# The within-chunk part of a chunked recurrence, cut into units of one head and two chunks and moved to other PSUM banks

## The chip, the cores and the metric

One core of a Trainium2 chip runs the whole program in one launch. The metric is the device time of that core in microseconds (us).

## What is computed

The program is two transformer blocks on 512 tokens of width 1024, in float32. The change lies in the second block, in a gated delta rule (a linear recurrence) with 8 heads that runs in both directions. A context of 256 tokens is scanned ahead of the 512, so a head has six chunks of 128 tokens: chunks 0 and 1 are the context, chunks 2 to 5 are the tokens whose outputs are wanted. In the reference, cut to what matters (its chunk is 64 tokens, the kernel's is 128):

```python
a_mat = where(strict, (kb @ k.T) * decay, 0.0)          # per head and chunk
t_mat = triangular_solve(eye + a_mat, eye)              # lower, unit diagonal
u, w  = t_mat @ vb, t_mat @ (kb * exp(gc))
qk    = where(tri, (q @ k.T) * decay, 0.0)
def step(s, inp):                                       # over the chunks, one after the other
    v_new = u_i - w_i @ s
    o_i   = qd_i @ s + qk_i @ v_new
    s     = s * gl_i + kd_i.T @ v_new
```

## The kernel before, in words

The function `gdn` works through the 8 heads as four pairs. For each pair four helpers run, and their order in the program is: `states(pair)`, `inputs(pair + 1)`, `output(pair)` (the loop at 1552; for the last pair `tail()`, which is projections of the next stage, stands in the place of `inputs`). Both directions of both heads go together, so there are four independent recurrences at a time.

`inputs` makes q, k and v of a pair: projections on TensorE (line 234, 235 and 237: every float32 product is three matmuls with operands split in a high and a low part) into `pg` banks; a convolution over tokens, of which ScalarE does the eviction (1247 and 1248) and a Silu (1256), and VectorE does the taps (1254, eight for a head of k or v, four for a head of q); and transposes on TensorE (1284) into `pt` banks, evicted by ScalarE (1286, 1289).

`states` has four parts:

- **The within-chunk part** (1358 to 1387). TensorE makes k k' and k q' for each chunk (1364, 1366) and, with a pair of matmuls (1373 a broadcast of decays, 1374 a mask), the exponent; ScalarE takes its Exp (1376); VectorE multiplies (1378 to 1380). The results are `M` and `E`, one each for a head and direction. The diagonal 32 by 32 blocks of `M` go to a tile `X`, by ScalarE copies (1384) and VectorE transposes (1386).
- **The inversion** of those blocks (1390 to 1404), a chain of small VectorE instructions, 31 steps, with a transpose of the whole at its start (1390) and two at its end (1403, 1404).
- **The merge** of the blocks to inverses of 128 by 128, small matmuls (1418 to 1458).
- **The chunk steps** (1461 to 1518), six of them: products with the state (1474, 1476), with the inverse (1488), the state's update (1501) and the output (1504).

`output` projects the gate z, squares and normalises the result (1533 to 1538), transposes it (1541), multiplies (1543) and stores it.

PSUM has eight banks: `pg` two, `pt` two and `sc` four. Before, the within-chunk part takes its products from `sc` banks, which the merge and the chunk steps use too, and its exponents from `pt` and `sc`. `M` and `E` lie in pages named `w`, taken anew for each pair.

No engine's order is written out by hand except SyncE's: a scheduler orders the instructions of the other engines ahead of time, by dependences and by the buffers that are free. On the chip each engine then takes its own list in that order, and waits at the head of it. SyncE's list (all loads of weights) is the program's order.

## Time and profile before

| | |
|---|---|
| median of 3 runs | 2312.93 us (2308.7 to 2313.16) |
| the profiled execution | 2312.48 us; its span 2310.7 us, so 1.8 us lie around the span |
| busy: TensorE, VectorE, ScalarE, GpSimd | 2192.4, 1211.8, 980.3, 263.1 us |
| the recurrence, from the gates to the last merge | about 1006 to 1410 us of the span |

Engines: PE is TensorE, PEld its weight loads, DVE VectorE, ACT ScalarE, POOL GpSimd. A row of the timeline has the start, the time from the first start to the last end, the engine and line, operation, tiles, shapes and, in brackets, how long the engine sat idle before it and what released it. Names of tiles are the program's names or those of its pools: `a` and `w` are pages, `gvn`, `gr` operands of the chunk steps, `inv` the tiles `X`, `L` and `Y` of the inversion, `whi` and `wlo` the split weights. A matmul's own duration is longer than its distance to the next; where a row merges several, the time beyond the first, divided by the others, is the distance.

### The profile page before, as it was taken

The numbers are of one execution on the slowest core, as the hardware profiler recorded it, in microseconds if no ns is written. First come the engines' busy times: TensorE is split into PE (matmuls) and PEld (weight loads), VectorE is DVE, ScalarE is ACT, GpSimd is POOL, SyncE is SP. The second block draws the span as 40 slices with busy tenths as digits, with TensorE's granted clock in tenths as the row PEclk, the third lists the DMA queues.
The fourth block names the chain that finished last, engine by engine and source line by source line (L and its number), as shares of the span: only waits on it lengthen the run. The fifth ranks groups of instructions, "written<-read, shape, count | busy, mean of one in ns | idle before, by whom it ended". The sixth has DMA issues, their size and how long they took to land.

```text
span 2310.7 us, 38251 instructions
## 1 busy us (share of the span) xinstructions
PE 2192.4 (95%) x15367; PEld 1947.6 (84%) x15367; DVE 1211.8 (52%) x2740; ACT 980.3 (42%) x2022; POOL 263.1 (11%) x435
## 2 busy tenths in 40 slices
PE   8999999998899999899989897999999998999999
PEld 8889988897779889767777787888898888898988
DVE  4554444555443233559596967436776454434343
ACT  4443244444333233565555553545555224314221
POOL 0221100001000001201111110301110001010112
PEclk9999999999999999999999998999999999999999
DMA  5234485465672232422121310240112542323232
GB/s 172 81 126 135 161 298 197 137 199 180 215 233 96 91 104 89 154 71 93 47 92 47 97 47 15 74 136 25 31 40 86 182 141 78 96 88 100 93 100 92
DMA packets 195817, 262.05 MB, mean 113 GB/s; under 512 B 12343, under 2 KB 157495, under 8 KB 195639
## 3 DMA queue, kind: packets, MB, share of 16 engines
q1 hardware_dynamic: 188864, 244.61, 32.7%
q10 hardware_dynamic: 6775, 15.00, 1.8%
q8 instruction: 120, 1.97, 0.4%
q14 instruction: 58, 0.48, 0.1%
HBM read 223.39 MB, written 36.18 MB: 112 GB/s over the span
## 4 chain that ended last, share of the span: by engine, by line
PE 75%; issue 9%; DMA 5%; DVE 4%; ACT 4%; POOL 2%; SPq 0%; ACTq 0%; POOLq 0%; DVEq 0%
PE pg L234 16%; PE pg L235 15%; PE pg L237 15%; PE sc L234 4%; PE sc L235 4%; PE sc L237 4%; DMA whi<-parts 2%; PE pg L223 1%; PE pg L224 1%; DMA parts<-fraw 1%; PE pg L225 1%; PE sc L1488 1%; DMA fraw<-in_w_in 1%; DMA wraw<-in_w_kv_mem 1%; DVE wlo L179 1%
## 5 line engine op out<-in xcount | busy, mean ns | idle before, releaser
L179 DVE TENSOR_TENSOR wlo<-wraw,whi 128x1024 fp32r<-128x1024 f32 (+2 forms) x267 | 325.6, 1222 | 405.9 <-ACT whi L178 401.2
L234 PE MATMUL pg<-xhi,whi 128*128 128x512 f32 (+1 forms) x1104 | 428.9, 392 | 30.4 <-DMA whi<-parts 12.9
L178 ACT ACTIVATE whi<-wraw 128x1024 fp32r<-128x1024 f32 (+2 forms) x267 | 275.6, 1035 | 417.0 <-PE pg L235 351.2
L235 PE MATMUL pg<-xlo,whi 128*128 128x512 f32 (+1 forms) x1104 | 426.1, 389 | 0.0
L237 PE MATMUL pg<-xhi,wlo 128*128 128x512 f32 (+1 forms) x1104 | 291.4, 384 | 1.0 <-DMA wlo<-parts 1.0
L234 PEld LDWEIGHTS pg<-xhi,whi 128*128 128x128 f32 x1104 | 211.3, 192 | 77.6 <-ACT whi L178 14.5
L235 PEld LDWEIGHTS pg<-xlo,whi 128*128 128x128 f32 x1104 | 211.3, 192 | 37.1
L237 PEld LDWEIGHTS pg<-xhi,wlo 128*128 128x128 f32 x1104 | 203.2, 190 | 41.0 <-DMA wlo<-parts 2.3
L234 PE MATMUL pg<-whi,xhi 128*128 128x256 f32 (+1 forms) x608 | 159.0, 291 | 0.5 <-ACT a L980 0.3
L235 PE MATMUL pg<-whi,xlo 128*128 128x256 f32 (+1 forms) x608 | 157.7, 290 | 0.0
L234 PE MATMUL sc<-whi,a 128*128 128x256 f32 x560 | 141.8, 285 | 1.6 <-ACT whi L178 1.6
L235 PE MATMUL sc<-whi,a 128*128 128x256 f32 x560 | 141.4, 284 | 0.0
L234 PE MATMUL pg<-whi,a 128*128 128x256 f32 x560 | 140.8, 283 | 0.0
L235 PE MATMUL pg<-whi,a 128*128 128x256 f32 x560 | 140.7, 283 | 0.0
L234 PEld LDWEIGHTS pg<-whi,xhi 128*128 128x128 f32 x608 | 118.9, 196 | 5.0 <-ACT whi L178 3.1
L235 PEld LDWEIGHTS pg<-whi,xlo 128*128 128x128 f32 x608 | 118.6, 195 | 1.1 <-issue 0.8
L237 PE MATMUL pg<-wlo,xhi 128*128 128x256 f32 (+1 forms) x608 | 104.3, 290 | 12.2 <-DVE wlo L179 12.2
L234 PEld LDWEIGHTS sc<-whi,a 128*128 128x128 f32 x560 | 107.8, 193 | 2.1 <-ACT whi L178 1.8
L235 PEld LDWEIGHTS sc<-whi,a 128*128 128x128 f32 x560 | 107.8, 192 | 0.2
L234 PEld LDWEIGHTS pg<-whi,a 128*128 128x128 f32 x560 | 107.5, 192 | 0.1
L235 PEld LDWEIGHTS pg<-whi,a 128*128 128x128 f32 x560 | 107.5, 192 | 0.0
L929 POOL TENSOR_TENSOR a<-a,a 128x256 f32<-128x256 f32 x64 | 48.9, 764 | 510.9 <-DVE a L928 510.2
(474 smaller groups left out, 4582.7 us busy)
## 6 DMA issues: line engine op xcount, KB each, us to landing
wraw<-in_w_in SPq DMA_DIRECT2D x56, 512.0 KB, 5.3
fraw<-in_w_mod SPq DMA_DIRECT2D x48, 512.0 KB, 5.6
parts<-fraw SPq DMA_DIRECT2D x48, 512.0 KB, 3.9
wraw<-in_w_gate_up SPq DMA_DIRECT2D x44, 512.0 KB, 4.8
wraw<-in_w_mlp_in SPq DMA_DIRECT2D x32, 512.0 KB, 3.8
wraw<-in_w_mlp_out SPq DMA_DIRECT2D x32, 512.0 KB, 3.6
whi<-parts SPq DMA_DIRECT2D x26, 512.0 KB, 4.0
wlo<-parts SPq DMA_DIRECT2D x26, 512.0 KB
```

The lines of the kernel that those rows point to most:

```text
L178: nc.scalar.activation(hi, raw, AF.Copy)
L179: self.wlo_eng.tensor_tensor(lo, raw, hi.bitcast(F32), op=OP.subtract)
L223: mm(out, a[0], b[0], start=start, stop=False)
L224: mm(out, a[0], b[1], start=False, stop=False)
L225: mm(out, a[1], b[0], start=False, stop=stop)
L234: mm(out, A[k][0], B[k][0], start=start and k == 0, stop=False)
L235: mm(out, A[k][late], B[k][1 - late], start=False, stop=False)
L237: mm(out, A[k][1 - late], B[k][late], start=False, stop=stop and k == n - 1)
L929: nc.gpsimd.tensor_tensor(self.x[t][:, cs], self.x[t][:, cs], u, op=OP.add)
L1488: mm(kv[h][:, d, 0], M[h, d][:, c], r[h, d], start=True, stop=True)
```

## The change

The within-chunk part is done in units of one head and two chunks (`a` = 0, 2, 4), for both directions at once. A unit takes one bank of `pg` for its products k k' and k q' and one of `pt` for its exponents, and none of `sc`. An exponent's matmul covers 256 columns for each direction, where it was 256 or 512 before; the multiplications on VectorE cover 256 columns each. `E` and `M` are now eight tiles (four each) that are taken once, ahead of the loop over the pairs, from new pages `m`; the list `w` gets shorter. The copies and transposes to `X` still come after the three units of a head. Lines of the changed kernel behind this part are smaller by 2, those of `inputs` larger by 1.

```diff
--- before.py
+++ after.py
@@ -21,7 +21,7 @@
 T = 512
 NEG = -1.0e30
 PHASE_A = dict(a=((4, 18), (2, 16)))
-PHASE_B = dict(a=((3, 14), (2, 9)), w=((3, 4), (2, 7), (1.5, 4), (1, 3)))
+PHASE_B = dict(a=((3, 14), (2, 9)), m=((3, 4), (2, 4), (1, 2)), w=((2, 4), (1.5, 4)))
 PHASE_C = dict(a=((6, 6), (4, 4), (3, 3), (2, 5)), t=((3, 3), (2, 8)))
 PHASE_D = dict(a=((4, 21), (2, 20)))
 BANKS_A = dict(pt=2, sc=3, fl=1)
@@ -1237,6 +1237,7 @@
         X, L, Y = (self.hb.tile([128, 32, 32], F32, name="inv", tag=f"inv{k}") for k in range(3))
         tm = [con.tile([128, 136], F32, name=f"invt{v}") for v in range(2)]
         nc.gpsimd.memset(X, 0.0)
+        E, M = ({(h, d): self.page([n, 128], s="m") for h in range(2) for d in range(2)} for n in (4, 6))
 
         def conv(ps, tile):
 
@@ -1355,36 +1356,33 @@
                 return slice(32 * b, 32 * b + 32)
 
 
-            E, M = {}, {}
             for h in range(2):
-                pg = [self.bank([128, n, 128], "sc") for n in (2, 4)]
-                pk = self.bank([128, 4, 128], "sc")
-                for c in range(6):
-                    k = kT[h][:, c]
-                    mm(pg[c >= 2][:, c - 2 * (c >= 2)], k, k, start=True, stop=True)
-                    if c >= 2:
-                        mm(pk[:, c - 2], k, qT[h][:, (c - 2) * 128:(c - 1) * 128], start=True, stop=True)
-                for d in range(2):
-                    i = d * 8 + h0 + h
-                    ec, e = self.page([2, 128], s="w"), self.page([4, 128], s="w")
-                    for a, n in ((0, 2), (2, 4)):
-                        pe = self.bank([128, n, 128], "sc" if a else "pt")
-                        pf = pe.rearrange("p a b -> p (a b)")
-                        mm(pf, sel[:, i:i + 1].to_broadcast([64, 128]), g["rows"][:, a * 128:(a + n) * 128], start=True, stop=False)
-                        mm(pe, idb, msk[:, d, None, :].to_broadcast([128, n, 128]), start=False, stop=True)
-                        for c in range(n):
-                            act((e if a else ec)[:, c], pe[:, c], AF.Exp, bias=nb[h][:, a + c, d:d + 1])
-                    m = self.page([6, 128], s="w")
-                    dve.tensor_tensor(m[:, :2], ec, pg[0], op=OP.mult)
-                    dve.tensor_tensor(m[:, 2:], e, pg[1], op=OP.mult)
-                    dve.tensor_tensor(e, e, pk, op=OP.mult)
+                for a in (0, 2, 4):
+                    kq = self.bank([128, 4, 128], "pg")
+                    pe = self.bank([128, 2, 2, 128], "pt")
+                    for c in (a, a + 1):
+                        k = kT[h][:, c]
+                        mm(kq[:, c - a], k, k, start=True, stop=True)
+                        if a:
+                            mm(kq[:, 2 + c - a], k, qT[h][:, (c - 2) * 128:(c - 1) * 128], start=True, stop=True)
+                    for d in D2:
+                        i = d * 8 + h0 + h
+                        mm(pe[:, d].rearrange("p a b -> p (a b)"), sel[:, i:i + 1].to_broadcast([64, 128]), g["rows"][:, a * 128:(a + 2) * 128], start=True, stop=False)
+                        mm(pe[:, d], idb, msk[:, d, None, :].to_broadcast([128, 2, 128]), start=False, stop=True)
+                    for d in D2:
+                        e = E[h, d][:, a - 2:a] if a else self.page([2, 128], s="m")
+                        for c in (a, a + 1):
+                            act(e[:, c - a], pe[:, d, c - a], AF.Exp, bias=nb[h][:, c, d:d + 1])
+                        dve.tensor_tensor(M[h, d][:, a:a + 2], e, kq[:, :2], op=OP.mult)
+                        if a:
+                            dve.tensor_tensor(e, e, kq[:, 2:], op=OP.mult)
+                for d in D2:
                     for b in range(4):
-                        xb, mb = X[blk(b), lane[h, d]], m[blk(b), :, blk(b)]
+                        xb, mb = X[blk(b), lane[h, d]], M[h, d][blk(b), :, blk(b)]
                         if d == 0:
                             act(xb, mb, AF.Copy)
                         else:
                             dve.transpose(xb, mb)
-                    E[h, d], M[h, d] = e, m
 
 
             dve.transpose(L, X.rearrange("p n i -> p i n"))
```

The scheduler's order changes with it, in each of the pairs. Three places, of the second pair (`inv` and the numbers behind a name, the buffer numbers, aside; `pg`, `pt`, `sc` are banks):

TensorE in the within-chunk part. Before (1373 and 1374 are the exponents, 234 to 237 projections of the pair after):

```order
L234 MATMUL pg<-xhi,whi 128x512
L1373 MATMUL pt<-rg,sel_7304 128x256
L1374 LDWEIGHTS idb
L1374 MATMUL pt<-gmask,idb 128x256
L235 MATMUL pg<-xlo,whi 128x512
L237 MATMUL pg<-xhi,wlo 128x512 x2
L1373 MATMUL sc<-rg,sel_7304 128x512
L1374 LDWEIGHTS idb
L1374 MATMUL sc<-gmask,idb 128x512
```

And now, from the transposes of the output (1539, before 1541) on:

```order
L1539 MATMUL pt<-ident,w_10595 128x128 x4
L1539 MATMUL pt<-ident,w_10596 128x128 x4
L1365 MATMUL pg<-a_10964 128x128 x2
L1370 MATMUL pt<-rg,sel_7304 128x256
L1371 LDWEIGHTS idb
L1371 MATMUL pt<-gmask,idb 128x256
L1370 MATMUL pt<-rg,sel_7304 128x256
L1371 LDWEIGHTS idb
L1371 MATMUL pt<-gmask,idb 128x256
L1365 MATMUL pg<-a_10964 128x128
L1367 MATMUL pg<-a_11125,a_10964 128x128
```

(`a_10964` and `a_11125` are k and q.) All 20 products and 24 matmuls of the exponents now stand in one row, with no projection between them; 25 projection matmuls stood between them before (36 of 256 columns in the last pair). In the first pair the six transposes of the gates' decays are still among them.

TensorE between the last chunk step and the transposes of the output. Before (1504 is the last step, the rows are the second half of the gate's projection):

```order
L1504 MATMUL sc<-gvn,w_10178 128x128
L1504 MATMUL sc<-gvn,w_10200 128x128
L237 MATMUL pg<-xhi,wlo 128x512 x4
L234 MATMUL pg<-xhi,whi 128x512
L235 MATMUL pg<-xlo,whi 128x512
```

Now (1502 is the last step; `hc` and the three rows ahead of it are the v projection of the second head, 1285 transposes of v, `xhi` with `whi` behind them the whole of the gate's projection):

```order
L1502 MATMUL sc<-gvn,m_9509 128x128
L237 MATMUL pg<-xhi,wlo 128x512 x3
L234 MATMUL pg<-hc,whi 128x256
L235 MATMUL pg<-hc,whi 128x256
...
L237 MATMUL pg<-hc,wlo 128x256 x4
L1285 MATMUL pt<-ident,a_11226 128x128 x6
L234 MATMUL pg<-xhi,whi 128x512
L235 MATMUL pg<-xlo,whi 128x512
```

Where 16 projection matmuls lay between the last step and the first transposes of the output (20 in the pairs after), 75 do now (51 of 512 columns, 24 of 256), with 12 transposes of v. The ones that are new here stood among the chunk steps before; those now have matmuls of about the same length there from the q and v projections, which stood beside the inversion and the merge before. In the last pair 174 projection matmuls stand between the output and the merge in both kernels; 36 of them stood inside the within-chunk part before, and all stand behind it now.

VectorE at the same place. Before, the normalisation of both heads stands in one row from the last step to the within-chunk part, and the taps of the next k (1254) begin with the inversion. Now there are two splits of the gate's weights (179) and the eight taps of v (1255) between the two heads:

```order
L1514 TENSOR_TENSOR w_10596<-w_10596,sc 128x128 x2
L1533 TENSOR_TENSOR on_11442<-on_11442,on_11441 128x4
L1535 TENSOR_TENSOR on_11443<-ors,qrs 128x4
L1536 TENSOR_TENSOR w_10595<-w_10595,on_11443 128x512
L1532 TENSOR_TENSOR on_12820<-qrs 128x4
L179 TENSOR_TENSOR wlo<-wraw,whi 128x1024 x2
L1255 SCALAR_TENSOR_TENSOR a_11291<-a_11290,convw,a_11291 128x254
L1255 SCALAR_TENSOR_TENSOR a_11291<-a_11290,convw,a_11291 128x510
```

The six taps of the next k that stood at the start of the inversion stand behind it, in all pairs that have one. In both kernels all multiplications of the within-chunk part stand behind the last chunk step and the output of the pair before on VectorE's list. SyncE's list is the same in both.

## Rows read from the trace of the kernel before

**Rows 1.** The page's chain that ended last, shares of the span.

```profile
PE 75%; issue 9%; DMA 5%; DVE 4%; ACT 4%; POOL 2%; SPq 0%; ACTq 0%; POOLq 0%; DVEq 0%
```

**Rows 2.** Windows cut at last step, inversion's start (L1390), merge's bulk; busy us, counts, clock, DMA.

```profile
core 0: us, PE busy (x) PEld busy (x) DVE busy (x) ACT busy (x) POOL busy (x), PEclk, DMA share, GB/s
...
1035.90:1068.00 32.10, 28.63 (x138) 23.30 (x138) 32.10 (x139) 7.12 (x12) 1.75 (x5) 0.95 0.51 165
...
1123.50:1153.70 30.20, 26.54 (x137) 20.01 (x136) 14.09 (x33) 16.39 (x54) 5.44 (x6) 0.94 0.27 88
...
1153.70:1187.10 33.40, 28.99 (x142) 23.65 (x140) 33.40 (x140) 8.54 (x16) 2.91 (x7) 0.95 0.47 158
...
1241.10:1270.40 29.30, 26.31 (x144) 20.11 (x143) 14.55 (x34) 16.02 (x52) 5.44 (x6) 1.00 0.27 91
...
1270.40:1301.80 31.40, 28.24 (x144) 23.32 (x144) 31.40 (x137) 8.62 (x17) 1.46 (x5) 0.95 0.55 177
...
1355.10:1381.60 26.50, 24.37 (x162) 20.38 (x162) 15.73 (x35) 15.98 (x52) 5.44 (x6) 1.00 0.20 61
...
1381.60:1410.30 28.70, 15.29 (x108) 14.55 (x108) 28.55 (x127) 5.13 (x11) 1.35 (x4) 0.73 0.11 29
```

**Rows 3.** Timeline of PE, from the second pair's last step to the last inversion.

```profile
1122.82 0.71 PE L1504 MATMUL sc<-gvn,w 128*128 128x128 f32 x4
...
1130.94 0.66 PE L1541 MATMUL pt<-ident,w 128*128 128x128 f32 x4 [2.33 <-DVE w L1538]
...
1143.01 1.16 PE L1364 MATMUL sc<-a 128*128 128x128 f32 x8 [0.16 <-ACT w L1376]
...
1184.30 0.82 PE L1284 MATMUL pt<-ident,a 128*128 128x128 f32 x6
...
1251.06 0.38 PE L1373 MATMUL pt<-rg,sel 64*128 64x256 f32 x1
...
1251.59 0.50 PE L1373 MATMUL sc<-rg,sel 64*128 64x512 f32 x1
...
1252.34 0.38 PE L1373 MATMUL pt<-rg,sel 64*128 64x256 f32 x1
...
1358.58 1.07 PE L237 MATMUL pg<-xhi,wlo 128*128 128x512 f32 x4
...
1387.58 0.63 PE L237 MATMUL pg<-wlo,hc 128*128 128x256 f32 x4
...
1404.24 1.22 PE L237 MATMUL pg<-wlo,xhi 128*128 128x256 f32 x4 [12.19 <-DVE wlo L179]
```

**Rows 4.** Timeline of ACT, from the first Exp of the first pair on.

```profile
1020.98 0.63 ACT L1376 ACTIVATE w<-pt,knb 128x128 f32<-128x128 f32 x2 [1.88 <-PE pt L1374]
...
1133.00 1.28 ACT L1376 ACT_TABLE_LOAD   x1 [5.20 <-DVE a L1543]
...
1140.57 1.49 ACT L1384 ACTIVATE inv<-w 32x192 f32<-32x192 f32 x4
...
1145.85 1.14 ACT L1376 ACTIVATE w<-sc,knb 128x128 f32<-128x128 f32 x4 [2.12 <-PE sc L1374]
...
1151.36 1.05 ACT L1248 ACTIVATE a<-pg,convw 128x256 f32<-128x256 f32 x2
...
1355.24 0.31 ACT L1533 ACTIVATE junk<-w 128x128 bf16<-128x128 f32 x1
...
1355.67 0.31 ACT L1533 ACTIVATE junk<-w 128x128 bf16<-128x128 f32 x1
...
1356.05 1.06 ACT L178 ACTIVATE whi<-wraw 128x1024 fp32r<-128x1024 f32 x1
```

**Rows 5.** Timeline of DVE, second pair: multiplication, transposes to `X`, a tap.

```profile
1143.59 0.41 DVE L1378 TENSOR_TENSOR w<-w,sc 128x256 f32<-128x256 f32 x1
...
1151.76 1.51 DVE L1386 STREAM_TRANSPOSE inv<-w 32x192 f32<-32x192 f32 x4
...
1157.56 0.74 DVE L1254 SCALAR_TENSOR_TENSOR a<-a,convw,a 128x510 f32<-128x510 f32 x1
```

## The prediction

> **What bounds the kernel now.** I read the chain of waits first: TensorE carries three quarters of it [rows 1], so the change can only pay where TensorE stands idle or runs slowly. Then the windows, cut at four events of each pair: the last chunk step, the start of the inversion on VectorE, the first bulk of the merge, and the next pair's last step. The chunk steps lie between these windows, and TensorE is nearly full there; the two windows shown for each pair are those in which it is not [rows 2]. From last step to inversion it is busy 26.5 of 30.2 us in the second pair, 26.3 of 29.3 in the third and 24.4 of 26.5 in the last; from inversion to merge 28.6 of 32.1, 29.0 of 33.4, 28.2 of 31.4, and in the last pair 15.3 of 28.7, at a granted clock of 0.73. The lines of VectorE and ScalarE in the same windows say what sets these lengths. During the inversion VectorE is busy all the time; ahead of it, VectorE is busy 14 of 30 us and ScalarE 16, so nothing is full, and a chain goes from engine to engine: TensorE waits 2.33 us for the normalised output [rows 3], ScalarE then loads the Exp table, and its Exps wait 2.12 us for a `pt` or `sc` exponent behind projections [rows 4]. The largest single idle time is 12.19 us in the last pair, for `wlo`, whose split sits behind the inversion on VectorE's list [rows 3].
>
> **The change part by part.** All times are within the profiled execution (2312.48 us, 0.45 below the median of the runs, 2312.93).
>
> *Work on TensorE.* The products are the same. For one head and direction the exponents were one pair of matmuls of 256 columns and one of 512, which take 0.53 and 0.75 us from start to start [rows 3], together 1.28; now it is three pairs of 256, 1.59. That is 0.31 x 16 = 5 us in all, or 1.2 us a pair. I cost it at nothing, since within this part the other two engines are slower; without that cover it is the 5 us. The projections are the same matmuls in another place.
>
> *The within-chunk part, first Exp to inversion.* Before it lasted from 1020.98 to 1035.9 in the first pair [rows 2, 4], 14.9 us, and some 18 us in the second, from 1135.4. Now no projection stands between its matmuls. ScalarE has 24 Exps, 0.26 us apart (1.14 for four, with the first longer), and eight copies, four in 1.49 [rows 4]: 24 x 0.26 + 3.0 = 9.2 us. Behind the last Exp come VectorE's last multiplications, at most four of 0.41, and four transposes of 1.51 together [rows 5]: 9.2 + 1.3 + 1.5 = 12.0. The row is not free of waits: the `pt` bank of unit n + 2 is that of unit n, and four copies of the first head stand in the middle of ScalarE's list, behind which a bank is held. I add 0.4 and take **12.4 us**. The lower end is 11, if the copies overlap the multiplications; the upper is the 14.9 us of the first pair before, in which only a few projections stood between.
>
> *From the last step to the first Exp.* Before: 1123.5 [rows 3] to about 1135.4, 11.9 us, or the window of 30.2 less the 18.3 that follow. Now TensorE first has 3 projections of 512 columns, 24 of 256, six transposes, 48 of 512, six transposes and eight more. By the distances in the rows, 0.227, 0.117 and 0.11 us [rows 3]: 0.7 + 2.8 + 0.7 + 10.9 + 0.7 + 1.0 = 16.8. There is one wait in it: the gate's projection needs the `pg` bank of v's, which ScalarE frees only after five squares of 0.43 behind the last step, two splits of 1.06, and the evictions of v, about 2.0 (twice the 1.05 that two of them take) [rows 4], some 6 us behind the last step, while TensorE is there at 4.2: 1.8 us idle, as the first two squares start early. That puts the second set of transposes of the output at 18.3 and their end at 18.8. Two VectorE multiplications, the store's issue and the table load of 1.28 [rows 4] follow: the first Exp at **21.5 us**, 9.6 later than before. In the last pair two more splits of weights stand ahead of it on ScalarE and VectorE, 1.3 us: 22.8. Lower end: 18, if the bank is free in time and v's taps and splits on VectorE (eight taps, two splits) do not delay the second head; upper: 25, with TensorE at its lower clock for a few us behind the idle time, as happens behind the 2.33 us in the second pair, whose window has a granted clock of 0.94 [rows 2].
>
> *The inversion.* The six taps at its start go behind it: two at 0.74 [rows 5], four of half that width or a little more, 3.0 us. They stand in the first three pairs only. What was hidden behind them is nothing; k's Silu and transposes come later, into the merge, where ScalarE has room. I take 3.0 off, with 0 and 4.6 as ends (the second pair's window is 2 us longer than the third's).
>
> *Chunk steps and merge.* They have the four `sc` banks to themselves now, but TensorE is nearly full there today; length as before, with 1.5 us either way for each of three pairs. The tail's matmuls are the same.
>
> **The sum.** First pair: 12.4 - 14.9 - 3.0 = -5.5. Second: 21.5 + 12.4 = 33.9 for 30.2, less 3.0: +0.7. Third: 33.9 for 29.3, less 3.0: +1.6. Last: 22.8 + 12.4 = 35.2 for 26.5 and no taps to lose: +8.7. Together +5.5, and 2312.5 + 5.5 = **2318 us**. As a check by TensorE's own work: beside the inversion it has 129 projection matmuls left, 24 us, and with the loads it waits for today (3 to 4 us) it is done about when the inversion is, so the inversion's window is the one that counts. In the last pair it is not work but the wait for `wlo` that sets it: the same 174 matmuls, the split in the same place behind the inversion. The idle time goes from 12.19 to perhaps 9, but the inversion itself begins 8.7 us later.
>
> So the part that the change is about does get shorter, by 2 to 6 us a pair. What is late next is its start: v and the gate now stand between the last step and the output, and the output holds the Exps.
>
> **The rivals.**
>
> *Faster, 2305.* The second half of the projections between the steps and the output costs less than I say: the wait for the `pg` bank does not arise, the clock stays up and the first Exp is at 18. That is 3.5 us in each of three pairs off my sum, 10.5, and with 11 instead of 12.4 for the row, 4 times 1.4, another 5.6: 2318 - 10.5 - 5.6 = 2302; half of the second, 2305. For it speaks that the idle times of 2.33 us (and two like it) for the output must go, since 75 matmuls now lie ahead of it; against it, that ScalarE's list is what it is. The Trainium skill ("Perfetto Trace Analysis", section Optimizing Scalar/DVE Operations) says that where these two engines are not saturated but cause bubbles on others, breaking up their instructions may let work complete sooner. By that rule alone the change pays: it is this case. It decides if the first Exp of the second pair lies under 19 us behind the last step.
>
> *Slower by much, 2332.* TensorE's clock falls in the row of units, since it waits there for one bank after another, in small pieces. The row has 20 x 2 x 0.13 + 12 x 0.53 = 11 us of matmuls at full clock [rows 3]; at half speed for a third of it, and for the projections behind, 3.5 us a pair, 14 us: 2332. For it: granted clocks of 0.94 and 0.95 in windows with 2 us of idle time, 0.73 with 12 [rows 2]. Against it: in the row TensorE is busy most of the time. The Trainium skill ("TensorE: Matmul & The Clock Gate", section A second HAM failure mode: psum-queue depth-cycling) tells of a kernel that cycled through PSUM banks and lost its clock by frequent short idling; by that rule this is the case to expect. It decides if the row's window shows a clock under 0.85.
>
> *No change, 2313.* What moves is hidden in both directions: VectorE's and TensorE's work in a period is the same, the inversion's start swings by a few us, and the steps give back what the output loses. And the change does not do what its tiles would allow, since the scheduler puts every multiplication behind the last step and the output: no part of the next pair starts early, in any pair.
>
> **How the numbers follow.** My forecast 0.40, faster 0.24, no change 0.20, slower by much 0.16. From low to high: 2302 is the faster case with all its terms, 2334 the slower one with 1.5 us of the steps; both ends are kept, as the unknown terms (first Exp 18 to 25, three times; row 11 to 14.9, four times; taps 0 to 4.6) reach as far. A measurement of this kernel can tell some 0.2%, 4.6 us. Forecast and slower case lie mostly above 2317; of the forecast a quarter falls under it. Faster 0.25, same 0.25, slower 0.50.
>
> **What would show it.** In the profile after: the first Exp of the second and third pair 20 to 23 us behind the last step; from there to the inversion 11 to 14 us in all pairs; no tap in the first two thirds of the inversion; in the first pair the merge 5 us earlier than now, counted from the gates; the wait for `wlo` in the last pair still 8 to 10 us. I am wrong if the steps get longer or shorter by over 2 us a pair, or if the first Exp comes under 19 us.

## The result, and the profile after

The changed kernel takes **2327.57 us** (2326.89 to 2328.87, 4 runs), against 2310.81 for the kernel before beside it: 1.0075 times as long, 95% interval 1.0058 to 1.0092. The same kernel on another chip gave 1.0072 (1.0058 to 1.0087). It is slower, by 16 to 17 us where 5.5 were forecast. The profiled span is 2326.8 us, 16.1 above that of before.

The chain that ended last, in the changed kernel: VectorE's share has more than doubled [rows 1].

```profile
PE 73%; DVE 9%; issue 9%; DMA 4%; ACT 3%; POOL 2%; SPq 0%; ACTq 0%; POOLq 0%; DVEq 0%
```

Windows of the changed kernel. For the first pair: from the gates to the first Exp, and from that Exp to the inversion. For the others: from the last step to the first Exp, and from there to the inversion. Two inversions and one stretch of merge and steps are shown too. I call the stretch from first Exp to inversion the row.

```profile
core 0: us, PE busy (x) PEld busy (x) DVE busy (x) ACT busy (x) POOL busy (x), PEclk, DMA share, GB/s
1008.00:1024.70 16.70, 10.62 (x50) 8.02 (x49) 4.39 (x22) 10.12 (x25) 0.00 (x0) 0.62 0.18 63
1024.70:1043.00 18.30, 17.11 (x60) 12.05 (x60) 10.43 (x29) 9.60 (x32) 0.00 (x0) 0.60 0.00 1
...
1123.30:1145.10 21.80, 19.90 (x113) 16.41 (x112) 10.76 (x22) 12.17 (x35) 5.43 (x6) 1.00 0.27 62
1145.10:1160.80 15.70, 13.07 (x54) 9.65 (x54) 10.41 (x29) 9.48 (x32) 0.00 (x0) 0.72 0.22 82
1160.80:1189.60 28.80, 25.60 (x133) 21.30 (x132) 28.77 (x132) 6.66 (x15) 0.00 (x0) 0.98 0.23 76
1189.60:1240.70 51.10, 48.73 (x633) 43.78 (x633) 39.27 (x117) 35.24 (x107) 15.11 (x30) 1.00 0.19 62
1240.70:1262.50 21.80, 19.92 (x113) 16.41 (x111) 10.76 (x22) 12.21 (x35) 5.44 (x6) 1.00 0.23 62
1262.50:1275.90 13.40, 10.77 (x58) 7.81 (x59) 10.41 (x29) 9.45 (x32) 0.00 (x0) 1.00 0.25 96
...
1359.10:1381.70 22.60, 20.68 (x116) 16.80 (x114) 13.11 (x24) 14.23 (x36) 5.64 (x7) 1.00 0.31 87
1381.70:1398.40 16.70, 14.25 (x65) 10.89 (x66) 10.39 (x28) 9.50 (x33) 0.00 (x0) 0.69 0.11 41
1398.40:1427.10 28.70, 21.99 (x169) 21.04 (x167) 28.58 (x127) 5.75 (x13) 0.93 (x3) 0.88 0.10 28
```

The same cuts in the kernel before, finer than in [rows 2]: the gates of the first pair, the second pair from its last step on, then the rows of the third and last pair.

```profile
1006.00:1021.00 15.00, 13.29 (x68) 10.67 (x68) 4.39 (x22) 10.16 (x26) 0.00 (x0) 0.77 0.21 70
...
1123.50:1135.40 11.90, 9.24 (x48) 7.40 (x46) 4.09 (x12) 4.87 (x19) 5.44 (x6) 0.86 0.69 222
1135.40:1153.70 18.30, 17.30 (x90) 12.61 (x91) 10.00 (x21) 11.53 (x36) 0.00 (x0) 1.00 0.00 0
...
1185.40:1241.20 55.80, 52.94 (x657) 47.63 (x656) 42.90 (x120) 41.36 (x126) 13.83 (x26) 0.97 0.01 2
...
1252.20:1269.90 17.70, 16.70 (x89) 12.37 (x89) 9.98 (x21) 11.48 (x37) 0.00 (x0) 1.00 0.01 5
...
1367.40:1381.60 14.20, 14.20 (x105) 12.35 (x104) 9.44 (x21) 9.70 (x34) 0.00 (x0) 1.00 0.13 48
```

Three things stand there. From last step to first Exp it is 21.8 us where it was 11.9. The row was full of TensorE's work at full clock before (17.30 of 18.30 us); now TensorE has 54 to 65 matmuls there instead of 75 to 105, and works at a granted clock of 0.60, 0.72 and 0.69 in three of four pairs. And the steps shown are shorter, with 24 matmuls fewer (x633 for x657).

Waits of TensorE in the changed kernel, by its timeline (start, length, in brackets the idle time before and what ended it):

```profile
1012.65 0.69 PE L1285 MATMUL pt<-ident,a 128*128 128x128 f32 x2 [1.87 <-ACT a L1290]
...
1019.87 1.46 PE L1224 MATMUL pt<-ident,a 128*64 128x128 f32 x6 [1.86 <-DVE g_nb L1212]
...
1128.38 0.50 PE L234 MATMUL pg<-xhi,whi 128*128 128x512 f32 x1 [0.88 <-ACT a L1249]
1135.31 0.87 PE L1285 MATMUL pt<-ident,a 128*128 128x128 f32 x6 [0.99 <-ACT a L1257]
...
1146.28 0.38 PE L1370 MATMUL pt<-rg,sel 64*128 64x256 f32 x1 [0.41 <-ACT m L1375]
...
1152.11 0.58 PE L1370 MATMUL pt<-rg,sel 64*128 64x256 f32 x1 [1.25 <-ACT m L1375]
...
1269.46 0.38 PE L1370 MATMUL pt<-rg,sel 64*128 64x256 f32 x1 [1.26 <-ACT m L1375]
...
1382.91 0.38 PE L1370 MATMUL pt<-rg,sel 64*128 64x256 f32 x1 [1.30 <-ACT m L1375]
...
1421.10 1.22 PE L237 MATMUL pg<-wlo,xhi 128*128 128x256 f32 x4 [5.37 <-DVE wlo L179]
```

Two short waits (0.88 and 0.99 us) lie ahead of the second pair's output. In the rows of the last three pairs an exponent waits 1.25 to 1.30 us for its `pt` bank, which an Exp frees that stands behind the four copies (or, in the last pair, behind the table load). The wait for `wlo` is 5.37 us, where it was 12.19 [rows 3].

By windows of 1 us the clock drops from 1.00 to 0.50 within about a us of that wait's end in the second and last pair, and not in the third. In the first pair it had dropped 12 us ahead of the row, at the wait of 1.87 us among the gates:

```profile
1012.00:1016.00 4.00, 1.60 (x7) 1.21 (x7) 0.69 (x3) 3.79 (x10) 0.00 (x0) 0.50 0.09 34
```

and it stays there until 1039 us, through two more waits of 1.74 and 1.86 us. In the kernel before it drops at the same place too, at a wait of 1.66 us, but 14 projections stand behind that wait, TensorE works without a break, and the clock is back at 1.00 ahead of the first Exp. Now no projection stands there (TensorE is busy 10.62 of 16.70 us, before 13.29 of 15.00).

Summed over the four pairs, from each profile's windows (us; the first column holds the gates in the first pair; "inversion" ends with its last transpose, "steps" with the last step):

| kernel | to first Exp | row | inversion | merge and steps | sum |
|---|---|---|---|---|---|
| before | 50.3 | 65.1 | 123.6 | 209.7 | 448.7 |
| after | 82.9 | 64.1 | 114.9 | 200.8 | 462.7 |
| after, other chip | 82.2 | 60.2 | 115.1 | 202.4 | 459.9 |
| units, `kk`/`kq` in `sc` | 52.0 | 57.7 | 119.3 | 209.5 | 438.5 |
| units, two `pg` banks a pair | 71.6 | 63.6 | 115.0 | 203.9 | 454.1 |
| whole heads, two `pg` banks a pair | 69.9 | 51.2 | 115.2 | 208.6 | 444.9 |

Sum of after less before: 14.0; the other 2.1 us lie ahead of the gates, in code that the change doesn't touch. The profile of the units in `sc` fell on the shortest of that kernel's twelve executions (2303.6 us, median 2313.5), that of whole heads with two `pg` banks on the longest of its six (2317.3, median 2307.6), so for their times the ratios below count, not the rows here.

Where the projections went, counted as the matmuls of lines 234, 235 and 237 in the same windows of the third pair (some records can be missing):

| kernel | to first Exp | row | inversion | merge and steps |
|---|---|---|---|---|
| before | 20 | 56 | 132 | 85 |
| units, `kk`/`kq` in `sc` | 38 | 35 | 121 | 98 |
| whole heads, two `pg` banks a pair | 55 | 27 | 122 | 88 |
| units, two `pg` banks a pair | 64 | 24 | 122 | 81 |
| after | 75 | 11 | 124 | 80 |

From run to run, the more `pg` banks the row takes (none, none, two, two and six a pair), the fewer projections run in it and the more stand ahead of the output.

### The profile page after: what moved, and what is told of

It reads as the page before. It is cut to its first block, busy times and chain, and to the rows that moved or that the text cites. A ratio compares the mean times of both kernels' runs of the same rounds, so it can differ in the third digit from the quotient of the medians.

```text
span 2326.8 us, 38368 instructions
## 1 busy us (share of the span) xinstructions
PE 2205.5 (95%) x15399; PEld 1960.4 (84%) x15399; DVE 1215.4 (52%) x2772; ACT 980.1 (42%) x2022; POOL 262.1 (11%) x435
## 4 chain that ended last, share of the span: by engine, by line
PE 73%; DVE 9%; issue 9%; DMA 4%; ACT 3%; POOL 2%; SPq 0%; ACTq 0%; POOLq 0%; DVEq 0%
PE pg L234 14%; PE pg L235 14%; PE pg L237 14%; PE sc L234 4%; PE sc L235 4%; PE sc L237 4%; DVE inv L1399 2%; DVE invt L1396 2%; PE pg L223 1%; PE pg L224 1%; DVE a L1255 1%; PE sc L1486 1%; PE pg L225 1%; DMA parts<-fraw 1%; DMA fraw<-in_w_in 1%
## 5 line engine op out<-in xcount | busy, mean ns | idle before, releaser
L234 PEld LDWEIGHTS pg<-xhi,whi 128*128 128x128 f32 x1104 | 210.3, 191 | 77.8 <-ACT whi L178 14.4
```

The lines of the kernel that those rows point to most:

```text
L234: mm(out, A[k][0], B[k][0], start=start and k == 0, stop=False)
```

## The experiments

My theory was the prediction's: the order (v and the gate ahead of the output) costs. All ratios are to the kernel before on the same chip, with 95% intervals; runs 1 to 4 shared a chip, 5 to 8, and 9 to 11. The letters A to F are explained where they first stand in an expectation.

**1. Only the tiles.** The form and banks of before, with `E`, `M` and the pages of the change:

```diff
-PHASE_B = dict(a=((3, 14), (2, 9)), w=((3, 4), (2, 7), (1.5, 4), (1, 3)))
+PHASE_B = dict(a=((3, 14), (2, 9)), m=((3, 4), (2, 4), (1, 2)), w=((2, 4), (1.5, 4)))
+        E, M = ({(h, d): self.page([n, 128], s="m") for h in range(2) for d in range(2)} for n in (4, 6))
...
-                    ec, e = self.page([2, 128], s="w"), self.page([4, 128], s="w")
+                    ec, e, m = self.page([2, 128], s="m"), E[h, d], M[h, d]
```

> The kernel before, with the change's tiles that stay for all pairs and its page sizes alone: heads, exponents and banks as before. Theory A (the cost is the order: the kk/kq products stand in `pg`, whose banks are handed out in the order of the program, so v and the gate go ahead of the output and the first Exp comes 10 us later): no unit, no `pg`, so 2311 us, within 4 of the kernel before, first Exp 11 to 12.5 us behind the last step. Theory B (the cost is TensorE's clock in the row of units): 2311 too. Theory C (the tiles themselves cost, by waits for pages that stay): 2318 or more, with new waits on M or E in the merge.

1.0001 (0.9985 to 1.0017). The tiles cost and bring nothing; C falls.

**2. The units, with their products in `sc`.**

```diff
-                    kq = self.bank([128, 4, 128], "pg")
+                    kq = self.bank([128, 4, 128], "sc")
```

> The change with one word undone: the kk/kq bank of a unit is an `sc` bank, so the units stay and the banks are no longer apart. A: the gate's projections go behind the Exps again, first Exp of the second and third pair 11 to 13 us behind the last step, row 14 to 17 us with projections in it, 2306 (2300 to 2313). C' (the cost is the smaller form: 5 us more on TensorE, copies in the middle): the cost stays, 2320 to 2328. B: projections stand between the units, so the clock holds at 0.95 or more in the row: 2306 to 2313, as A; the windows' clock tells, not the time.

0.9982 (0.9967 to 0.9998): the whole cost of the change is gone. The windows of the second pair, last step to first Exp and the row:

```profile
1119.70:1130.60 10.90, 8.55 (x46) 6.60 (x44) 4.07 (x12) 4.35 (x15) 5.43 (x6) 1.00 0.74 235
1130.60:1145.40 14.80, 14.80 (x83) 11.18 (x83) 10.25 (x29) 10.10 (x34) 0.00 (x0) 1.00 0.02 6
```

Projections stand in the row again, TensorE is busy for all of it, and the clock holds. So units as such need not cost (C' had 2320 or more); units that ask for `pg` do.

**3. The converse: whole heads, k q' products in `pg`.** On top of 1:

```diff
-                pk = self.bank([128, 4, 128], "sc")
+                pk = self.bank([128, 4, 128], "pg")
```

> The converse: the form of before (a head and all its chunks, larger exponents) with tiles that stay, and only its k-q products moved to a `pg` bank. A: the order tips without any unit: first Exp 18 us or later behind the last step, 2320 to 2330. C': no unit, so no cost: 2311 within 4. B: the row has no projections in it either, so the clock may fall to 0.6 to 0.8 there; if it is the clock alone that costs, the time is 2316 to 2322.

0.9964 (0.9951 to 0.9978), faster than before; every theory had it slower or equal. Windows of the first pair's row, then of the second, third and last pair:

```profile
1029.60:1044.10 14.50, 14.50 (x44) 9.17 (x45) 9.33 (x20) 9.33 (x32) 0.00 (x0) 0.61 0.01 1
...
1130.20:1148.10 17.90, 17.89 (x101) 14.67 (x99) 9.35 (x21) 11.74 (x36) 4.66 (x6) 1.00 0.33 91
1148.10:1160.40 12.30, 11.88 (x59) 8.75 (x59) 9.36 (x21) 9.39 (x34) 0.00 (x0) 1.00 0.22 84
...
1261.80:1274.00 12.20, 11.79 (x59) 8.71 (x59) 9.34 (x21) 9.29 (x33) 0.00 (x0) 1.00 0.25 93
...
1374.80:1387.00 12.20, 11.33 (x78) 9.44 (x78) 9.34 (x20) 9.22 (x32) 0.00 (x0) 1.00 0.16 58
```

The order did tip: the first Exp is at 17.9 us. But TensorE works 17.89 of those 17.90 us, and the row that follows is 12.3 us long, nearly full and at full clock. So a late first Exp need not cost, if TensorE works meanwhile and gets the time back later. That refutes A as I had put it. (In the first pair the clock had dropped among the gates, at 1020 us, as in the change.)

**4. Filling the row with six more products a unit.**

```diff
+                    fl = self.bank([128, 4, 128], "sc")
+                    for c in range(6):
+                        mm(fl[:, c % 4], kT[h][:, a], kT[h][:, a], start=True, stop=True)
```

> The change, with six more products of 128 columns for each unit (k by k of the unit's first chunk, into an `sc` bank that nobody reads): 36 a pair, 36 x 0.11 = 4.0 us of TensorE's work, in the row and ahead of it; nothing of the result changes. B: the clock holds (0.9 or more) in all four rows, which become 13.5 to 15 us instead of 18.3, 15.7, 13.4 and 16.7, and the kernel gets faster for it by some 4 to 8 us: 2319 to 2324. A alone (the clock costs nothing, a chain from engine to engine sets the row): the work comes on top, 2328 to 2340.

1.0058 (1.0042 to 1.0074), 2328.6 us. The clock is 1.00 in all four rows, as B said, but the rows are 14.6, 17.9, 17.9 and 17.1 us, three of them longer than B allowed. The filling was twice what the expectation says: a product of 128 columns stands as two matmuls on TensorE, so a unit's six are twelve, and 36 a pair take 72 x 0.11 = 8 us, not 4.0. The second pair's row, and one stretch of filling (16 matmuls in 1.95 us):

```profile
1137.70:1155.60 17.90, 17.90 (x122) 14.97 (x121) 10.61 (x29) 9.70 (x32) 0.00 (x0) 1.00 0.20 75
```

```profile
1138.74 1.95 PE L1374 MATMUL sc<-a 128*128 128x128 f32 x16
```

TensorE is busy for all of that row: the filling ate what the clock gave. The clock is B's, the time lies at the low end of A's range; the run doesn't tell them apart.

**5. The change again, with three edits of it beside it.**

> The changed kernel itself once more, as a measure for the three beside it, and for what the clock does. The ratio to the kernel before is 1.0075 again (1.005 to 1.010, so 2327 to 2333 on this chip). Theory B (the clock falls in the row because TensorE waits there for banks): the row's clock is below 0.8 in at least two of the four pairs, and a row with the clock up lasts 13.4 us again, one with it down 15.5 us or more. If all four rows have a clock above 0.95 and the time is the same, B falls.

1.0072; rows of 16.7, 13.4, 13.4 and 16.7 us at clocks of 0.69, 1.00, 1.00 and 0.69. So the clock is down for much of the first and last pair's row in both profiles, and of the second pair's in one of two, at the same waits. In the first pair it had dropped among the gates again, at 1012 us; here it came back a us ahead of the first Exp and dropped again at 1026.

**6. Copies behind both heads.**

```diff
-                for d in D2:
+            for h in D2:
+                for d in D2:
                     for b in range(4):
                         xb, mb = X[blk(b), lane[h, d]], M[h, d][blk(b), :, blk(b)]
```

> The change, with the copies and transposes into X behind both heads' units, so that no copy stands on ScalarE between Exps. The bank hold (theory D: TensorE waits 1.3 us a pair for a `pt` bank behind those copies, and the clock falls behind that wait): no idle time over 0.5 us in the row, clock above 0.9 in all four, rows 12.5 to 13.5 us, together 12 us less than in the change: 2316 (2312 to 2320). If the hold matters but not for the clock: 4 us less at most, less the 1.5 us a pair by which eight copies at the end are longer than four: 2326 to 2331. The first Exp is at 21.8 us as in the change, in either case.

1.0058 (1.0044 to 1.0072), a change of 0.14% with overlapping intervals. The wait of 1.25 us is gone in the second and third pair and their rows are 12.9 us. In the first and last the clock fell all the same:

```profile
1031.60:1048.30 16.70, 15.30 (x59) 11.11 (x60) 10.22 (x29) 9.48 (x32) 0.00 (x0) 0.69 0.00 1
...
1384.60:1402.10 17.50, 15.28 (x65) 11.66 (x66) 10.33 (x29) 9.50 (x33) 0.00 (x0) 0.61 0.11 41
```

So the copies are worth half a us a pair, and the wait behind them is not what takes the clock in those two pairs. In the last one it drops at a wait that the copies have no part in, the one for the `pt` bank whose Exp stands behind the table load:

```profile
1385.82 0.58 PE L1370 MATMUL pt<-rg,sel 64*128 64x256 f32 x1 [1.32 <-ACT m L1375]
```

D, which put it down to the copies, falls; that a wait for a `pt` bank can take the clock does not.

**7. Filling with three products a unit**, as in 4 with `range(3)`.

> As the run with six more products for each unit, but with three: 18 a pair, 2.0 us of TensorE's work, 14 of them between the first head's units. B: clock 0.9 or more in the rows, which last 14 to 15.5 us instead of 13.4 to 18.3, and the time is 3 to 5 us under that of the change on the same chip. A alone: 2 to 8 us over it.

1.0051 (1.0037 to 1.0065), 2324.75 us against 2330.79 for the change beside it: 6 us less, with 4 us a pair more to do (by the count of run 4, not the 2.0 of the expectation). Last pair, to the first Exp and the row:

```profile
1358.00:1380.70 22.70, 21.75 (x127) 18.11 (x126) 13.11 (x24) 14.32 (x37) 5.64 (x7) 1.00 0.32 87
1380.70:1395.00 14.30, 13.06 (x91) 10.70 (x90) 10.48 (x28) 9.38 (x32) 0.00 (x0) 1.00 0.13 48
```

The rows are 15.7 (clock 0.71), 15.5, 15.2 and 14.4 us (all 1.00). It is B's direction, but the two intervals overlap, and the rows, 60.8 us in sum, are no shorter than the 60.2 of run 5's profile. That useless work shortens the program, so that TensorE's state in the row has a price, is likely by this run and not shown.

**8. `sc` in the last pair alone.**

```diff
-                    kq = self.bank([128, 4, 128], "pg")
+                    kq = self.bank([128, 4, 128], "pg" if pair < 3 else "sc")
```

> The change, with the kk/kq bank of the units in `sc` in the last pair alone. A (the lateness of the Exps is mostly given back within the next period in the first three pairs, and paid in full in the last, where nothing is left to give it back): first Exp of the last pair 12 to 14.5 us behind the last step, row 14.5, so 10.5 us less than the change, 2317 on a chip where the change takes 2327.6. If it is paid in equal parts in every pair, a quarter of the whole: 3 to 5 us less, 2323. The wait for `wlo` in the last pair grows from 5.4 to 10 us again, and costs nothing more.

1.0054 (1.0040 to 1.0068), 4 us less than run 5 by the medians, not 10.5; that is the size of the expectation's other case, but the two intervals overlap. The windows of the last pair:

```profile
1357.80:1380.40 22.60, 21.65 (x127) 18.01 (x126) 13.11 (x24) 14.23 (x36) 5.64 (x7) 1.00 0.32 86
1380.40:1395.00 14.60, 14.60 (x106) 12.59 (x106) 10.26 (x29) 10.16 (x35) 0.00 (x0) 1.00 0.13 49
```

The row is full and at full clock again, 2.1 us shorter, with 71 projections in it, but the first Exp is as late as ever, with 75 ahead of it. So what stands ahead of the output in one pair is decided earlier than in its own row. As I read the order, it is the work that could not run in the row before. A is wrong there too. The wait for `wlo` grew to 11.3 us.

**9 to 11. `wlo` of the last pair's tail on GpSimd**, on top of 2, 3 and 1:

```diff
         def tail():
+            self.wlo_eng = nc.gpsimd
             self.latent = self.mla_latent(H, HC, w)
```

> The run with the kk/kq bank in `sc` in all pairs, with one thing more: the weight splits of the last pair's tail (the subtraction that makes `wlo`) go to GpSimd, which stands idle through the inversion, so they no longer stand behind the inversion on VectorE's list. The `wlo` wait of 10.4 us goes; a split takes 3.1 us there instead of 1.2 (by 0.76 for 128x256 on GpSimd), four of them before the merge, 12.5 us, and TensorE has 227 projection matmuls beside the inversion in place of 153. Theory E (TensorE's idle and half-speed time is the whole difference between these kernels): 6 to 10 us less than without it, 2303 to 2308 on a chip where before takes 2314. If what follows the inversion is bound by something else, the same time as without it.

> The same edit on the run with the form of before and only the k-q products in `pg`: E: its idle time in the last inversion is 10.6 us (18.53 busy of 29.1), so 6 to 10 us less than without it, ratio to the kernel before 0.992 to 0.994.

> The same edit on the form of before with standing tiles, which took the same time as the kernel before: how much of the two runs beside it is GpSimd's part alone. E: the wait of 12 us goes, so 7 to 11 us less: ratio 0.995 to 0.997. If the units in `sc` are worth nothing by themselves, this run is as fast as the one with the kk/kq bank in `sc` and GpSimd; if they are worth what TensorE's idle time says (before 8.5 + 3.3 us idle and 4.4 lost to the clock between last step and inversion in all pairs, against 5.3 + 1.0 and none), that one is 6 to 10 us faster than this.

1.0007 (0.9995 to 1.0019), 0.9968 (0.9953 to 0.9983), 1.0005 (0.9990 to 1.0020): no gain on any of the three. The two splits beside the last inversion, in the first of these (view of the line, from 1380 us on: min, median and max of the duration in ns), and TensorE's wait:

```profile
L179 POOL TENSOR_TENSOR wlo<-wraw,whi x2: 2376/6607/10838, 1390.3 to 1401.1; 128x1024 fp32r<-128x1024 f32 x2
```

```profile
1401.15 1.22 PE L237 MATMUL pg<-wlo,xhi 128*128 128x256 f32 x4 [9.29 <-POOL wlo L179]
```

Both ran beside VectorE's inversion. The first took 10.84 us and the second 2.38, and the inversion grew from 28.7 to 30.9 us. In this run and in 10 the wait kept 9.29 and 8.47 us under another name. In run 11 it did go, from 12.21 us in run 1's profile to 1.50, and another of 5.60 for the inversion stands behind it:

```profile
1391.44 0.75 PE L237 MATMUL pg<-wlo,xhi 128*128 128x256 f32 x4 [1.50 <-POOL wlo L179]
...
1411.38 0.39 PE L1417 MATMUL sc<-inv,m 32*32 32x32 f32 x4 [5.60 <-DVE inv L1402]
```

There the last pair's way to the first Exp, its row and its inversion are 3.0, 0.8 and 2.0 us longer than in run 1's profile. So E is not borne out, and what the `wlo` wait is worth without these costs stays open. The runs also repeat 2 and 3 with GpSimd's splits on top: with units in `sc` the kernel is 0.9982 or 1.0007 of before, which is no difference that these runs settle; with whole heads and two `pg` banks it is faster both times.

**12. Units, with two `pg` banks a pair instead of six.**

```diff
-                for a in (0, 2, 4):
-                    kq = self.bank([128, 4, 128], "pg")
+                pk = self.bank([128, 4, 128], "pg")
+                for a in (0, 2, 4):
+                    kk = self.bank([128, 2, 128], "sc")
...
-                            mm(kq[:, 2 + c - a], k, qT[h][:, (c - 2) * 128:(c - 1) * 128], start=True, stop=True)
+                            mm(pk[:, c - 2], k, qT[h][:, (c - 2) * 128:(c - 1) * 128], start=True, stop=True)
```

> The change's units, with the banks of the run that was fastest so far: the k-q products of a head's four chunks in one `pg` bank, so that a pair asks for two `pg` banks in the row instead of six, and each unit's two kk products in an `sc` bank. Theory F (what costs is that every unit asks for a `pg` bank: the projections, which need the same two banks, cannot run in the row or beside its start, and TensorE stands or runs at half speed there; the smaller form itself is harmless): first Exp 17 to 19 us behind the last step, rows 13 to 15 us at a clock of 0.95 or more, no wait of over 0.5 us between last step and first Exp, ratio to the kernel before 0.995 to 0.999. Theory C' (the small form costs, by 5 us of TensorE's work and its waits): 1.003 or more, as the change. The kernel with the form of before and these banks has 0.9964.

1.0028 (1.0014 to 1.0041): between F and C', so both hold in part. First Exp at 18.7 us in the second and third pair, with no wait, as F said. The rows, first to last pair:

```profile
1023.30:1041.90 18.60, 18.60 (x60) 12.82 (x61) 10.23 (x29) 9.58 (x32) 0.00 (x0) 0.60 0.00 1
...
1142.40:1155.80 13.40, 12.59 (x66) 9.53 (x66) 10.20 (x28) 9.49 (x32) 0.00 (x0) 1.00 0.22 84
...
1256.20:1271.20 15.00, 14.19 (x66) 10.66 (x66) 10.20 (x28) 9.51 (x33) 0.00 (x0) 0.89 0.19 71
...
1374.20:1390.80 16.60, 15.73 (x79) 12.48 (x79) 10.22 (x29) 9.52 (x33) 0.00 (x0) 0.69 0.12 45
```

Against 3, where the products' banks are of the same kinds, units take 13.4 us for 12.3 at full clock, and lose the clock in the third and last pair; in the first pair it had dropped among the gates in both runs, and the rows are 18.6 and 14.5 us. From the change to this run the part to the first Exp gets 11.3 us shorter (table); from this run to 3, the row gets 12.4 us shorter. The ratios step by 0.0047 and 0.0064, 11 and 15 us.

The first step is the `pg` banks' alone. The second is not the smaller form's alone: whole heads have their exponents in `pt` and `sc`, units in `pt` only, and the one wait of TensorE that the timeline shows in the last three rows of units, with the clock's drop behind it in the third and last pair, is for such a bank:

```profile
1148.96 0.38 PE L1371 MATMUL pt<-rg,sel 64*128 64x256 f32 x1 [0.81 <-ACT m L1376]
...
1262.78 0.38 PE L1371 MATMUL pt<-rg,sel 64*128 64x256 f32 x1 [0.81 <-ACT m L1376]
```

Units with exponents in `sc` as well were not run, so what is the form's and what is the exponents' banks' stays open. (Of these two waits of equal length, the second was followed by the lower clock and the first wasn't.)

## Why the prediction was right and wrong

The sign and the range held, and the likeliest case was the right one in its place: what is late next is the start of the Exps. The size was a third of what came, because two terms of the sum were mis-sized in opposite directions, by 14.5 and 9.0 us; that they cancel in part is luck. Of the signs that the prediction gave, those on the first Exp and on the taps came true and three failed: rows of 11 to 14 us (three of four are longer), an earlier merge in the first pair (it is later), and a wait of 8 to 10 us for `wlo` (5.37). By its own words it is wrong if the steps change by over 2 us a pair, and in two pairs they did.

- **From the last step to the first Exp: right.** 21.8, 21.8 and 22.6 us, forecast 21.5, 21.5 and 22.8. The wait for the `pg` bank was 0.88 us instead of 1.8, but a second of 0.99 stood behind it, for v's Silu.
- **The inversion: right.** 2.9 to 3.0 us shorter in the first three pairs, as forecast.
- **The within-chunk part, first Exp to inversion: this step failed.** Forecast 12.4 four times, 49.6 us; measured 64.1, so 14.5 us too low (60.2 and 10.6 in run 5's profile). At full clock it is 13.4 (third pair), 1.0 more each time: I had added 0.4 for the banks, and one wait alone is 1.26 us. The rest, 10.5 us, stands in the three rows with a low clock, 18.3, 15.7 and 16.7. That was the case "slower by much", with a clock under 0.85 as its sign; I gave it 0.16 and priced the forecast as if none of it happened. Its mechanism, a wait for a bank in the row, fits the second and last pair, 5.6 us. In the first pair, 4.9 us, the clock had dropped among the gates, where I forecast no change. The Trainium skill ("TensorE: Matmul & The Clock Gate", section A second HAM failure mode: psum-queue depth-cycling) describes a clock lost to small idle times between groups that cycle through banks. In the second and last pair the trace agrees, from 1.00 to 0.50 at waits of 1.25 and 1.30 us; the third pair waits 1.26 us and keeps its clock. The forecast and this rival do not exclude each other: I should have put a part of its price into the sum.
- **Chunk steps and merge unchanged: wrong too.** 4.4 and 4.8 us shorter in the first two pairs, 1.0 longer in the third, 0.8 shorter in the last: 9 us together that came back. I had written that the steps get as many matmuls from q and v as they lose; in the second pair they have 81 projections for 95 before, and 24 matmuls fewer in all, while 75 for 20 stand behind them, ahead of the output. So the steps give back a part of what the output loses, as the rival "no change" had it.
- **No work in the row.** I took the projections to be "the same matmuls in another place". The place counts. The row is a stretch in which a chain from engine to engine leaves TensorE free, and projections that run there are nearly free: run 2's third row holds 35 of them in 14.7 us, the change's 11 in 13.4, both at full clock. With six `pg` banks taken a pair, those of the next pair run there only behind the last unit; the third row holds 11 for 56, and the stretch ahead of the output, where TensorE is full, 75 for 20. Runs 2 and 12 show it by giving the banks back: all of the cost goes with six, 11 us with four. Run 8 shows that a pair's own row does not decide how much stands ahead of its output. In the first pair the same loss, of 14 projections among the gates, goes with a clock that stays down for 27 us.
- **The rival "faster"** rested on breaking up ScalarE's and VectorE's instructions, for which the Trainium skill ("Perfetto Trace Analysis", section Optimizing Scalar/DVE Operations) speaks. No run here bears it out. With two `pg` banks (runs 3 and 12, which differ in the exponents' banks too) VectorE is busy 10.2 us in a row of units and 9.35 in one of whole heads, and the units' row is longer, 13.4 for 12.3. With all products in `sc` (runs 1 and 2) the units' row is shorter, 14.7 for 18.2, with fewer projections in it, and the times, 1.0001 and 0.9982 of before, are not apart beyond their intervals. That the tiles should let parts start early didn't come to pass in any pair.
- **Readings of the prediction that were off and weigh little.** The third pair's window of 29.3 us ends 0.5 us behind the start of the inversion (1269.93). The row's matmuls, 20 x 2 x 0.13 + 12 x 0.53, are 11.6 us, not 11. The windows with clocks of 0.94 and 0.95 have 3.2 to 4.4 us of idle time, not 2.

Sum, by these terms: 5.5 forecast, 14.5 for the row, 9.0 back from the steps, 0.4 for the first Exps, 1.7 longer from the gates to the first Exp in the first pair, 2.1 ahead of the gates: 5.5 + 14.5 - 9.0 + 0.4 + 1.7 + 2.1 = 15.2 of the 16.1 us. Of the rest 0.5 is the third pair's window and 0.3 the inversion.

What stays open: what decides in which pair the clock falls, as the same order of instructions kept it in one execution and lost it in another; how the 15 us from run 12 to run 3 divide between form and exponents' banks; and what the last pair would gain without its wait for `wlo`. The kernel of run 3 (with run 10, the same but for GpSimd's splits) is the fastest measured here, faster than both.

## What to carry to other kernels

When a change gives a latency-bound stretch banks of its own, ask whose banks they were, and what else ran in that stretch thanks to sharing: independent work was nearly free there, and cost in full where TensorE was already busy. Count a moved matmul by where TensorE would else stand, not by its length. And where a change takes the filling out of a row of small matmuls, price that row at both clocks before calling it shorter, and look ahead of the row too: a clock that drops there can stay down through it. Whole heads with larger instructions, and exponents spread over more banks, beat units here by 1.1 us a row at full clock, and kept the clock in every row that they began with it.

## What the runs showed of the hardware that was not expected

TensorE's granted clock in the last pair of the changed kernel, in two neighbouring windows of 2 us, the first with the wait of 1.30 us at 1382.91 in it:

```profile
1382.00:1384.00 2.00, 1.09 (x6) 0.71 (x7) 1.41 (x4) 1.89 (x8) 0.00 (x0) 1.00 0.74 283
1384.00:1386.00 2.00, 2.00 (x10) 1.63 (x8) 0.86 (x3) 1.14 (x4) 0.00 (x0) 0.51 0.00 0
```

It goes from the upper level (2.4 GHz) to the lower (1.2), and a matmul of 128 columns then stands 0.21 us from the next instead of 0.11; by the same view it is back at 1.00 from 1396 us on, 2.4 us ahead of the row's end. With six products more a unit it was 1.00 in every pair's row, at 14.6 to 17.9 us for the row. It doesn't follow the waits alone: one of 1.26 us in the third pair of the same execution, and one of 0.81 us in run 12, left it at 1.00, while another of 0.81 us in run 12 was followed by 0.50. And in run 9 a row that was full of work was 17.7 us long, for 14.8 in run 2, as the clock had dropped ahead of it, behind waits of 1.72 and 0.62 us, and came back only 5 us behind the first Exp.

GpSimd's first subtraction of 128x1024 beside the inversion of run 9 took 10.84 us, where two ahead of the inversion took 2.35 and 2.36. VectorE's small multiplications went on at their usual length meanwhile, until two of them took 4.73 us together (two of the same width just ahead took 0.41), while the second subtraction ran in 2.38:

```profile
1398.80 4.73 DVE L1400 TENSOR_TENSOR inv<-inv,invt 128x96 f32<-128x96 f32 x2
```

The Trainium skill ("SBUF — State Buffer", section SBUF: two separate sides) tells of a port pair that VectorE and GpSimd share, and says that one blocks the other when VectorE reads two operands from SBUF and GpSimd reads SBUF too. The inversion's multiplications and the subtraction do, and by that the trace agrees: each engine stood while the other ran, by these lengths first GpSimd for some 8 us, then VectorE for some 4.
